# A second sequence's down projection as seven block products on one Trainium2 core, with their operand sums made in the stage before it

## The chip, the core and the metric

The program runs on one core of a Trainium2 chip. The core has five instruction queues that run side by side: TensorE (matrix products, called PE in the profile, with its weight loads as PEld), VectorE (DVE), ScalarE (ACT), GpSimd (POOL) and SyncE (SP), which here issues every transfer between the chip's memory and the on-chip buffers. The metric is the time of one execution on the device in microseconds (us), lower is better.

## The reference

One transformer-like layer is applied to two sequences, a sample of 512 tokens and a prompt of 1024 tokens, with the same weights (width 1024, feed-forward width 2816 = 22 x 128):

```python
def trunk(x, c, ...):
    ...
        mod = (c_act @ w_mod[l] + b_mod[l])[:, None, :]
        ...
        z = h @ w_in[l]
        ...
        mix = jnp.concatenate([rmsnorm(attn, g_attn_out[l]), rmsnorm(lru, g_lru_out[l])], axis=-1)
        x = x + gt1 * (mix @ w_out[l])
        h = rmsnorm(x, g_norm2[l]) * (1.0 + sc2) + sh2
        gu = h @ w_ffn_in[l]
        g_, u_ = jnp.split(gu, 2, axis=-1)
        x = x + gt2 * ((jax.nn.silu(g_) * u_) @ w_ffn_out[l])
    return rmsnorm(x, g_final)
```

The part that changes is the prompt's down projection `(silu(g) * u) @ w_ffn_out`, of size 1024 x 2816 x 1024, and what stands ahead of `mix @ w_out`.

## The kernel before

**Layout.** Activations stand transposed, features on the 128 partitions, tokens along the free side in chunks of 512: the sample is one chunk, the prompt two (0 and 1). A tile is 128x512. Every float32 matrix is split into a high and a low part of a rounded type (`whi`/`wlo` of a weight, `hh`/`hl`, `ach`/`acl`, `mxh`/`mxl` of activations), and one product of tiles is three matmuls (`mm3`): high by high, high by low, low by high. Making a high part is one copy on ScalarE (now and then on VectorE), a low part one subtraction on VectorE.

**Order.** Nothing is scheduled by the compiler. `Plan` (from line 90) keeps an estimated clock for each engine; `weave` (line 400) runs a main generator of matmuls and, at each of its yields, first emits drains that are due (`side.fast`), then the weight loader's steps (`pump`, line 338), then steps of background generators (`side.gens`) whose inputs the plan says are ready. `finish` (line 391) emits all that is left of a background generator before the main program goes on. What comes out is a fixed order on each engine, and each engine works through its own queue in order. `estimate` (line 99) gives the plan's costs: a float32 matmul of 512 columns counts 4 x 512 / 2400 = 0.853 us.

**Stages of the second half.** The sample's gate and up stage and the first half of its down projection (`ffn_out_half`) run while the prompt's recurrent unit (`lru`) and attention are worked off beside them. `s_lru` and `s_att` (lines 1524 and 1525) are two chains that end with `mix_lru` and `mix_att` of both prompt chunks: the squares of the four tiles are summed, `rstd` adds them over the partitions with two matmuls by `ones_h` (tiles `ssh`, `ssl`), then comes a root on ScalarE, four reciprocals on VectorE (`bc`), a scaling of each tile and its split into `mxh`, `mxl`. `side.finish(s_lru, s_att)` stands ahead of `out_main(1, 0, ...)`, the output projection of the prompt's chunk 0.

Then follow the output projections of chunks 0 and 1 (8 units of 24 matmuls each), the other half of the sample's down projection, and the prompt's gate and up stage `ffn_in_seven` (line 1239). It already multiplies by Strassen's scheme in Winograd's form: for each of 22 feature tiles j seven products of 12 matmuls make the gate and up tiles of both chunks; VectorE adds the products from PSUM, and the result tiles are stored to memory (`ac<-v`, `ac<-u`), 44 in all. Its seven right-hand operand sets (`ops`, 56 tiles) stay in a heap of 72 tiles (`N_HEAP`).

The prompt's down projection `ffn_out` (line 1371) then runs once for each chunk: 22 steps j, each with one weight tile pair (128x1024) and one activation tile, which `act_reader` loads and splits three steps ahead; 8 output tiles sit in 8 PSUM banks. `down` adds each output tile to the residual, squares it, and `final` (line 1421) normalises and stores. For chunk 1 the squares of the eight tiles are not summed on VectorE but given to TensorE as eight float32 matmuls by `ones_d`.

## Time and profile before

| what | us |
|---|---|
| median of 3 runs | 1638.21 (1635.48 to 1639.18) |
| the profiled execution, its own time | 1637.11 |
| its span, from the first instruction to the last | 1635.3 |
| TensorE busy | 1581.5 (97%) |
| VectorE busy | 1148.4 (70%) |
| ScalarE busy | 793.4 (49%) |
| prompt's gate and up stage (953.42 to 1373.48) | 420.06 |
| prompt's down projection (1373.48 to 1613.74) | 240.26 |

A matmul is listed with its latency (about 0.39 us), while the next one starts much earlier, so TensorE's busy time says that it had work, and the starts in the timeline say how fast it went. In tables by windows a number in parentheses is a count of instructions, PEclk is the granted TensorE clock as a share of full speed (0.50 is the lower level, 1.2 GHz of 2.4), and DMA is the mean busy share of the 16 DMA engines.

### The profile page before, as it was taken

The page shows a single profiled execution, that of the slowest core. Times are in us where ns is not written, and L with a number is a line of the kernel's source. Part 1 is how long each engine was busy: PE and PEld are TensorE (multiplying, and loading weights), DVE is VectorE, ACT ScalarE, POOL GpSimd, SP SyncE. Part 2 cuts the span into 40 slices and gives each one's busy share as a digit, 9 for nine tenths or more (in the row PEclk, how much of TensorE's full clock was granted, in tenths as well). Part 3 has the DMA queues.
Part 4 walks back from the last instruction along what each step waited for, and adds up shares of the span by engine and source line. Part 5 has one row for each costly group of instructions (what it writes and reads, how often), then busy time and mean ns, then how long its engine had stood idle before and what let it go on. Part 6 is the DMA issues. An engine that isn't in the chain of part 4 may idle for free.

```text
span 1635.3 us, 19943 instructions
## 1 busy us (share of the span) xinstructions
PE 1581.5 (97%) x7120; PEld 1273.0 (78%) x7120; DVE 1148.4 (70%) x1846; ACT 793.4 (49%) x1257; POOL 98.6 (6%) x148
## 2 busy tenths in 40 slices
PE   7999999999999999999699999999999999999996
PEld 1777888678678888888588888888888888888884
DVE  5787777637779897988857997666666666337334
ACT  3556786425985858665435643223222223334321
POOL 0000221000021120212000000000000000000000
PEclk9999999999999999999899999999999999999998
DMA  9674224475533333344365433222222226454541
GB/s 336 226 255 145 97 91 135 166 253 180 168 114 112 123 116 104 127 150 127 114 230 190 133 127 112 78 77 85 90 88 86 78 78 210 134 184 156 185 148 52
DMA packets 104787, 231.36 MB, mean 141 GB/s; under 512 B 10992, under 2 KB 17904, under 8 KB 104688
## 3 DMA queue, kind: packets, MB, share of 16 engines
q1 hardware_dynamic: 104688, 230.09, 42.6%
q8 instruction: 56, 0.92, 0.2%
q14 instruction: 43, 0.35, 0.1%
HBM read 189.16 MB, written 40.89 MB: 141 GB/s over the span
## 4 chain that ended last, share of the span: by engine, by line
PE 82%; ACT 7%; DVE 6%; DMA 2%; issue 2%; SPq 0%; DVEq 0%; ACTq 0%
PE pm L61 54%; PE ps L61 28%; ACT ga L61 2%; ACT gi L61 1%; ACT gs L61 1%; DMA mst<-w_mod 1%; DVE lh L61 1%; DVE bc L61 1%; DVE hl L61 1%; DVE x L61 1%; DVE wlo L61 0%; ACT L61 0%; SPq L61 0%; DVE ao L61 0%; DMA qf<-zq 0%
## 5 line engine op out<-in xcount | busy, mean ns | idle before, releaser
L61 PE MATMUL pm<-hh,whi 128*128 128x512 f32 x688 | 275.8, 401 | 0.2 <-DVE hh L61 0.2
L61 PE MATMUL pm<-hh,wlo 128*128 128x512 f32 x688 | 270.5, 393 | 2.1 <-DVE wlo L61 2.1
L61 PE MATMUL pm<-hl,whi 128*128 128x512 f32 x688 | 270.6, 393 | 0.5 <-DVE hl L61 0.5
L61 ACT ACTIVATE whi<-wst 128x1024 fp32r<-128x1024 f32 x134 | 141.2, 1056 | 210.7 <-PE pm L61 105.8
L61 DVE TENSOR_TENSOR wlo<-wst,whi 128x1024 fp32r<-128x1024 f32 x162 | 198.4, 1226 | 54.6 <-ACT whi L61 52.7
L61 PEld LDWEIGHTS pm<-hh,whi 128*128 128x128 f32 x688 | 130.6, 190 | 30.9 <-issue 4.4
L61 PEld LDWEIGHTS pm<-hh,wlo 128*128 128x128 f32 x688 | 130.3, 189 | 30.7 <-DVE wlo L61 2.5
L61 PEld LDWEIGHTS pm<-hl,whi 128*128 128x128 f32 x688 | 130.4, 190 | 25.9 <-DVE hl L61 1.1
L61 PE MATMUL pm<-ach,whi 128*128 128x512 f32 x352 | 138.3, 393 | 1.4 <-DVE sg L61 1.4
L61 PE MATMUL pm<-ach,wlo 128*128 128x512 f32 x352 | 137.1, 390 | 0.0
L61 PE MATMUL pm<-acl,whi 128*128 128x512 f32 x352 | 137.1, 390 | 0.0
L61 DVE TENSOR_TENSOR acl<-ac,ach 128x512 fp32r<-128x512 f32 x88 | 60.8, 696 | 81.9 <-ACT ach L61 80.8
L61 POOL TENSOR_SCALAR sx<-sx,es 128x384 f32<-128x384 f32 (+1 forms) x96 | 74.6, 794 | 255.5 <-DVE es L61 161.3
L61 ACT ACTIVATE ach<-ac 128x512 fp32r<-128x512 f32 x84 | 52.2, 628 | 64.4 <-DMA ac<-ac 62.8
L61 PEld LDWEIGHTS pm<-ach,whi 128*128 128x128 f32 x352 | 66.1, 188 | 15.2 <-DVE sg L61 1.8
L61 PEld LDWEIGHTS pm<-ach,wlo 128*128 128x128 f32 x352 | 66.1, 188 | 14.0
L61 PEld LDWEIGHTS pm<-acl,whi 128*128 128x128 f32 x352 | 66.1, 188 | 13.3 <-issue 0.2
L61 PE MATMUL pm<-mxh,whi 128*128 128x512 f32 x192 | 76.2, 397 | 0.0
L61 PE MATMUL pm<-mxl,whi 128*128 128x512 f32 x192 | 75.3, 392 | 0.0
L61 PE MATMUL pm<-mxh,wlo 128*128 128x512 f32 x192 | 75.3, 392 | 0.0
L61 DVE SCALAR_TENSOR_TENSOR x<-pm,modT,x 128x512 f32<-128x512 f32 x40 | 29.6, 745 | 56.8 <-PE pm L61 56.7
L61 PE MATMUL ps<-acl,whi 128*128 128x512 f32 x176 | 68.5, 389 | 0.0
(252 smaller groups left out, 3416.4 us busy)
## 6 DMA issues: line engine op xcount, KB each, us to landing
wst<-w_f SPq DMA_DIRECT2D x154, 512.0 KB, 3.7
mst<-w_mod SPq DMA_DIRECT2D x96, 256.0 KB, 5.4
ac<-ac SPq DMA_DIRECT2D x88, 256.0 KB, 4.1
wst<-w_in SPq DMA_DIRECT2D x28, 512.0 KB, 4.5
wst<-w_out SPq DMA_DIRECT2D x24, 512.0 KB, 3.7
x<-x_p SPq DMA_DIRECT2D x32, 256.0 KB, 5.5
xm<-x SPq DMA_DIRECT2D x24, 256.0 KB, 2.0
x<-xm SPq DMA_DIRECT2D x24, 256.0 KB, 6.0
```

Source lines behind the costliest of these rows:

```text
L61: r = fn(*args, **kw)
```

## The change

- **Down projection.** `ffn_out` is gone. `ffn_out_seven` computes both chunks at once by seven products: the 22 feature tiles are cut into two halves of 11, the 1024 outputs into two halves of 4 tiles. A product is 11 steps of 4 output tiles of 3 matmuls, 132 matmuls, into 4 PSUM banks (`pm` and `ps` in turn). After each product its four sums go to the residual tiles by VectorE (`p1` to `p7`).
- **Left sums.** `left_sums` is a background generator of the gate and up stage: for each of 11 pairs of weight tiles it loads four 128x512 blocks (`wd`), makes four sums on VectorE and stores them to memory (`s1`, `s2`, `d3`, `d4`), from where the last four products fetch them.
- **Right sums.** The gate and up stage goes through j in the order 0, 11, 1, 12, ... and after each pair `lean` makes four differences on VectorE (`t1` to `t4`); all seven right-hand sets go to memory, 77 tiles. `act_reader` reads them back four steps ahead.
- **Norms.** `s_lru` and `s_att` end with chunk 0's norm. Chunk 1's (`s_mix`) is made beside chunk 0's output projection, and finished ahead of chunk 1's.
- **End.** In the last product each output tile's squares are kept apart only for the last four tiles; the others are summed into one.
- **Plan.** A float32 matmul with 32 output rows (`mst,caw`, the modulation's product in strips) counts 0.15 us instead of 0.853.

The diff, cut to its core:

```diff
             four = op == "matmul" and kw["rhs"].dtype == F32
-            cost = max(4 * n, 515) / 2400 if four else max(n, 256 if op == "transpose" else 128) / 2400 + 0.0133 * (op == "matmul")
+            strip = four and outs[0].shape[0] == 32
+            cost = 0.15 if strip else max(4 * n, 515) / 2400 if four else max(n, 256 if op == "transpose" else 128) / 2400 + 0.0133 * (op == "matmul")
...
+            b[j // half, c] = d[v]
+            if j // half or c == 0:
+                yield d[v],
+                self.sp.dma_start(out=right[("11", "21")[j // half] if c == 0 else "22"][j % half], in_=d[v])
+            if key == (j % half + half, 1):
+                soon(lean(j % half, b[0, 0], b[0, 1], b[1, 0], b[1, 1]))
+
+        def lean(j, b11, b12, b21, b22):
+
+            yield b11, b12, b21, b22
+            t = {}
+            for n, x, y in (("t3", b22, b12), ("t1", b12, b11), ("t2", b22, "t1"), ("t4", b21, "t2")):
+                t[n] = self.T(n)
+                self.dve.tensor_tensor(out=t[n], in0=x, in1=t.get(y, y) if isinstance(y, str) else y, op=ALU.subtract)
+                yield t[n],
+                self.sp.dma_start(out=right[n][j], in_=t[n])
...
+        for j in (j for i in range(half) for j in (i, i + half)):
...
+    def left_sums(self, left):
+
+        def one(j):
+            a = []
+            for o in (0, NFF // 2):
+                for h in range(2):
+                    t = self.T("wd")
+                    self.sp.dma_start(out=t, in_=self.a["w_f2"][j + o, :, h * CH:(h + 1) * CH])
+                    a.append(t)
+            a11, a21, a12, a22 = a
...
+            yield a21, a22, a11
+            s3 = self.T("wd")
+            tt(out=s3, in0=a11, in1=a21, op=ALU.subtract)
+            yield s3,
+            store("d3", s3)
...
-    def ffn_out(self, seq, R, W, get, late, end, ahead, done):
+    def ffn_out_seven(self, seq, Rs, W, right, get, made, done):
...
+        def p7(m, ps, free):
+            yield lambda: at[m] == 6, ps
+            self.dve.tensor_tensor(out=u[m], in0=u[m], in1=ps, op=ALU.add)
+            free()
+            yield u[m],
+            onto(0, m + half, u[m])
+            yield from square(0, m + half)
+            left[0] -= 1
+            onto(1, m + half, u[m])
...
+        order = (("11", p1), ("21", p2), ("t4", p4), ("t2", p6), ("t3", p7), ("t1", p5), ("22", p3))
+        for p, (key, after) in enumerate(order):
...
+            cut = n - 3 if last else n - 1
+            if p == 2:
+                self.side.finish(made)
+            for j in range(cut):
+                take(j)
+                if p == 0 and j >= 2 and j - 2 < KT:
+                    for c in range(2):
+                        x[c][j - 2] = self.T("x")
+                        self.sp.dma_start(out=x[c][j - 2], in_=Rs[c]["dram"][j - 2])
+                for m in range(half):
+                    share(j, m)
...
-        s_lru = side.add(chain(self.lru(1, 2, zP, Lp, SQp), *(self.mix_lru(c, Lp, SQp, mixP[c]) for c in range(2))))
-        s_att = side.add(chain(self.attention(1, 2, zP, AOp), *(self.mix_att(c, AOp, mixP[c]) for c in range(2))))
+        s_lru = side.add(chain(self.lru(1, 2, zP, Lp, SQp), self.mix_lru(0, Lp, SQp, mixP[0])))
+        s_att = side.add(chain(self.attention(1, 2, zP, AOp), self.mix_att(0, AOp, mixP[0])))
...
         side.finish(s_lru, s_att)
+        s_mix = side.add(chain(self.mix_lru(1, Lp, SQp, mixP[1]), self.mix_att(1, AOp, mixP[1])))
         side.weave(out_main(1, 0, mixP[0], RP[0]))
+        side.finish(s_mix)
...
+        s_left.append(side.add(self.left_sums(left)))
+        side.weave(self.ffn_in_seven(W, ops, right, lambda: reads.append(self.act_reader(right["11"], 4))))
         ops.clear()
-        for c in range(2):
-            side.weave(self.ffn_out(1, RP[c], W, reads.pop(0), 2 * c, c == 1, read(1) if c == 0 else lambda: None, done_p(c)))
+        side.weave(self.ffn_out_seven(1, RP, W, right, reads.pop(), s_left[0], done_p))
```

How the orders move, at three places. First TensorE at the start of the prompt's output projection, before (`ach,whi` is the end of the sample's down projection, `ones_h` the sum of squares of a norm, `mxh,whi` the output projection):

```order
L61 MATMUL pm_6838<-ach_7574,whi_7339 128x512
L61 MATMUL pm_6838<-acl_7589,whi_7339 128x512
L61 MATMUL pm_6838<-ach_7574,wlo_7379 128x512
L61 MATMUL ps_7683<-ssh_7679,ones_h_91 128x512 [waits PE_49,Activation_49]
L61 MATMUL ps_7683<-ssl_7681,ones_h_91 128x512 [waits DVE_49]
L61 MATMUL pm_7726<-mxh_7652,whi_7425 128x512
L61 MATMUL pm_7726<-mxl_7660,whi_7425 128x512
```

The same place in the changed kernel:

```order
L61 MATMUL pm_6924<-ach_7607,whi_7418 128x512
L61 MATMUL pm_6924<-acl_7609,whi_7418 128x512
L61 MATMUL pm_6924<-ach_7607,wlo_7426 128x512
L61 MATMUL pm_7706<-mxh_7647,whi_7480 128x512 [waits DVE_49,Activation_49]
L61 MATMUL pm_7706<-mxl_7649,whi_7480 128x512
L61 MATMUL pm_7706<-mxh_7647,wlo_7495 128x512
L61 MATMUL pm_7706<-mxh_7651,whi_7480 128x512 [waits Activation_49]
L61 MATMUL pm_7706<-mxl_7660,whi_7480 128x512 [waits DVE_49]
```

The sum of squares of chunk 1's attention no longer stands ahead of the output projection; it comes 146 rows later, and the projection's first matmuls now wait for chunk 0's own split tiles.

Second VectorE in the middle of one feature tile of the prompt's gate and up stage, before (`u`, `v`, `w`, `p1` are sums of products, `slo`, `dlo`, `glo` low parts of weights, `wdif`, `wsum` weight sums):

```order
L61 TENSOR_TENSOR p1_9875<-p1_9875,ps_9903 128x512 [waits PE_49]
L61 TENSOR_TENSOR slo_9934<-wsum_9885,shi_9926 128x1024 [waits Activation_49]
L61 TENSOR_TENSOR w_9943<-u_9894,ps_9918 128x512 [waits DMAHW7_49,PE_49]
L61 TENSOR_TENSOR u_9894<-v_9910,ps_9918 128x512 [waits DVE_49]
L61 TENSOR_TENSOR wdif_9947<-wst_9821,wst_9835 128x512
```

The same place in the changed kernel, in the first part of that stage, with what now stands ahead of it:

```order
L61 TENSOR_TENSOR t2_9778<-u_9601,t1_9767 128x512 [waits DMAHW1_49,DVE_49]
L61 TENSOR_TENSOR t4_9788<-v_9628,t2_9778 128x512 [waits DMAHW3_49,DVE_49]
L61 TENSOR_TENSOR v_9791<-u_9769,ps_9757 128x512 [waits DMAHW4_49,PE_49]
L61 TENSOR_TENSOR wd_9793<-wd_9728,wd_9730 128x512 [waits DMAHW6_49,DMAHW5_49]
L61 TENSOR_TENSOR wd_9730<-wd_9730,wd_9734 128x512 [waits DMAHW0_49,DVE_49]
L61 TENSOR_TENSOR wd_9728<-wd_9730,wd_9728 128x512 [waits DVE_49]
L61 TENSOR_TENSOR p1_9745<-p1_9745,ps_9780 128x512 [waits PE_49]
L61 TENSOR_TENSOR wd_9732<-wd_9732,wd_9728 128x512 [waits DMAHW7_49,DVE_49]
L61 TENSOR_TENSOR slo_9823<-wsum_9747,shi_9813 128x1024 [waits Activation_49]
L61 TENSOR_TENSOR w_9841<-u_9769,pm_9805 128x512 [waits DMAHW2_49,PE_49]
```

Left sums and right differences stand between the sums of the products, and some of them wait for loads; here a feature tile is 17 instructions of VectorE's queue before and 25 now; the left sums are all made in the first nine of the 22 feature tiles, and after that a tile is 17 and 21 instructions in turn.

Third ScalarE at the end of the sample's norms, ahead of its output projection, before (`mrow` is the copy of a modulation row that TensorE waits for, `mxh` a high part for the output projection):

```order
L61 ACTIVATE mxh_2879<-lh_2376 128x512 [waits DMAHW6_49,DVE_49]
L61 ACTIVATE mrow_2887<-ps_2850 128x512 [waits DMAHW6_49,PE_49]
L61 ACTIVATE zo_2896<-pm_2817 128x512 [waits PE_49,Activation_49]
L61 ACTIVATE whi_2899<-wst_2218 128x1024
L61 ACTIVATE mxh_2901<-lh_2718 128x512 [waits DVE_49]
L61 ACT_TABLE_LOAD
L61 ACTIVATE bc_2903<-ps_2884,eps_93 128x512 [waits PE_49]
L61 ACTIVATE mxh_2963<-ao_1734 128x512 [waits DMAHW0_49,DVE_49]
```

The same place in the changed kernel:

```order
L61 ACTIVATE mxh_3022<-lh_2520 128x512 [waits DVE_49,Activation_49]
L61 ACTIVATE mxh_3032<-lh_2821 128x512 [waits DMAHW5_49,DVE_49]
L61 ACT_TABLE_LOAD [waits PE_49]
L61 ACTIVATE bc_3062<-ps_3049,eps_194 128x512 [waits Activation_49]
L61 ACT_TABLE_LOAD
L61 ACTIVATE zo_3082<-pm_2973 128x512
L61 ACTIVATE zo_3085<-pm_3040 128x512 [waits DMAHW7_49,PE_49]
L61 ACTIVATE mxh_3092<-ao_1852 128x512 [waits DVE_49,Activation_49]
```

The modulation's copy has moved ahead of the four `mxh<-lh`, and the attention's root and its table load now follow all four of them; on TensorE 18 matmuls stand between this norm's two matmuls by `ones_h` and the first matmul of the output projection, where before there were 48.

## Rows read from the trace of the kernel before

**Rows 1.** The page: span, TensorE's busy time, chain that ended last by engine.

```profile
span 1635.3 us, 19943 instructions
PE 1581.5 (97%) x7120; PEld 1273.0 (78%) x7120; DVE 1148.4 (70%) x1846; ACT 793.4 (49%) x1257; POOL 98.6 (6%) x148
PE 82%; ACT 7%; DVE 6%; DMA 2%; issue 2%; SPq 0%; DVEq 0%; ACTq 0%
```

**Rows 2.** Windows: length, busy PE, PEld, DVE, ACT, POOL; PEclk, DMA share, GB/s.

```profile
953.42:1373.48 420.06, 420.06 (x1850) 347.33 (x1851) 290.35 (x392) 127.35 (x165) 2.75 (x2) 1.00 0.29 94
1373.48:1613.74 240.26, 240.26 (x1059) 198.62 (x1058) 101.82 (x118) 78.49 (x99) 3.43 (x2) 1.00 0.47 153
900.00:940.00 40.00, 40.00 (x178) 33.14 (x177) 39.76 (x58) 26.90 (x42) 0.00 (x0) 1.00 0.40 130
```

**Rows 3.** TensorE's timeline at the end: start, length, instruction, count.

```profile
1613.52 0.39 PE L61 MATMUL ps<-ach,wlo 128*128 128x512 f32 x1
1613.74 7.03 PE L61 MATMUL ps<-sqt,ones_d 128*128 128x512 f32 x16
```

**Rows 4.** ScalarE's timeline at the end: the last tile's square.

```profile
1614.73 0.63 ACT L61 ACTIVATE sqt<-x 128x512 f32<-128x512 f32 x1 [2.03 <-DVE x L61]
```

**Rows 5.** TensorE's timeline at the prompt's output projection; in brackets the idle time before.

```profile
789.62 0.39 PE L61 MATMUL pm<-ach,wlo 128*128 128x512 f32 x1
802.36 0.79 PE L61 MATMUL ps<-ssh,ones_h 128*128 128x512 f32 x1 [12.35 <-ACT ssh L61]
803.68 0.63 PE L61 MATMUL pm<-mxh,whi 128*128 128x512 f32 x1
806.93 0.39 PE L61 MATMUL pm<-mxh,wlo 128*128 128x512 f32 x1
```

**Rows 6.** Windows of 5 us in that gap.

```profile
795.00:800.00 5.00, 0.00 (x0) 0.00 (x0) 4.30 (x8) 4.27 (x8) 0.00 (x0) 0.50 0.01 3
```

**Rows 7.** VectorE's timeline of chunk 0's attention norm.

```profile
780.06 0.69 DVE L61 TENSOR_TENSOR ssl<-sqt,ssh 128x512 fp32r<-128x512 f32 x1 [1.32 <-ACT ssh L61]
783.92 3.39 DVE L61 RECIPROCAL bc<-bc 128x128 f32<-128x128 f32 x4 [1.43 <-ACT bc L61]
789.09 2.73 DVE L61 SCALAR_TENSOR_TENSOR ao<-ao,vec,bc 128x512 f32<-128x512 f32 x4
796.96 2.49 DVE L61 TENSOR_TENSOR mxl<-ao,mxh 128x512 fp32r<-128x512 f32 x4
```

**Rows 8.** ScalarE's timeline of the same norm: table load and root.

```profile
781.90 1.28 ACT L61 ACT_TABLE_LOAD   x1 [1.35 <-PE ps L61]
783.19 0.69 ACT L61 ACTIVATE bc<-ps,eps 128x512 f32<-128x512 f32 x1
```

**Rows 9.** Who TensorE waited for, whole span: us in total, times, longest.

```profile
PE ps L61 <- ACT ssh L61: 12.4, 1, 12.4
PE ps L61 <- ACT mrow L61: 7.9, 4, 3.4
```

**Rows 10.** Windows of 6 us after two of the waits for `mrow`.

```profile
302.00:308.00 6.00, 6.00 (x18) 5.03 (x19) 5.04 (x9) 3.40 (x4) 0.00 (x0) 0.50 0.56 184
448.00:454.00 6.00, 6.00 (x25) 4.65 (x24) 5.96 (x14) 1.75 (x3) 2.79 (x4) 0.72 0.00 0
```

**Rows 11.** TensorE's timeline: one modulation product in strips, 8 matmuls as 16.

```profile
440.06 1.92 PE L61 MATMUL ps<-mst,caw 128*32 128x512 f32 x16
```

**Rows 12.** Groups by form, VectorE in the gate and up stage: busy, mean ns, idle.

```profile
L61 DVE TENSOR_TENSOR wsum<-wst 128x512 f32<-128x512 f32 x21 | 14.4, 684 | 0.0
L61 DVE TENSOR_TENSOR slo<-wsum,shi 128x1024 fp32r<-128x1024 f32 x21 | 25.6, 1220 | 0.5 <-ACT shi L61 0.5
```

**Rows 13.** DMA issues of the page: count, KB each, us to landing.

```profile
wst<-w_f SPq DMA_DIRECT2D x154, 512.0 KB, 3.7
ac<-ac SPq DMA_DIRECT2D x88, 256.0 KB, 4.1
```

**Rows 14.** A window at the start in which TensorE waited for loads.

```profile
20.00:40.00 20.00, 17.25 (x51) 4.71 (x49) 18.30 (x31) 3.06 (x5) 0.00 (x0) 0.97 0.98 365
```

More of the change, by code (lines that the diff above doesn't have):

```diff
@@ L1237, in ffn_in, with ffn_in_seven @@
                 W.free(*w)
-    def ffn_in_seven(self, W, ops, acts, ahead):
+    def ffn_in_seven(self, W, ops, right, ahead):
         def product(w, o, key):
@@ L1259, in add @@
         def add(d, ps, to, of):
-            d.setdefault(to, self.T(to) if to != of else d[of])
+            if to not in d:
+                d[to] = self.T(to)
             self.dve.tensor_tensor(out=d[to], in0=d[of], in1=ps, op=ALU.add)
@@ L1301, in ffn_in_seven @@
             W.free(*S)
[L1302 removed]
+            soon(gated(d, 6, *(yield from product((U, None), 0, "t4")), [("v", "v")], "p", "v", (j, 0)))
             W.free(U)
[L1304 removed]
+            soon(gated(d, 7, *(yield from product(D, 1, "22")), [("w", "w")], "w", "u", (j, 1)))
             W.free(*D)
@@ new lines, in left_sums @@
+    def left_sums(self, left):
[7 more added lines that the diff above has]
+            a11, a21, a12, a22 = a
+            tt = self.dve.tensor_tensor
+            sl = slice(j % 2 * CH, (j % 2 + 1) * CH)
+            store = lambda n, t: self.sp.dma_start(out=left[n][j // 2][:, sl], in_=t)
+            yield a21, a22, a11
[3 more added lines that the diff above has]
+            store("d3", s3)
+            tt(out=a21, in0=a21, in1=a22, op=ALU.add)
+            yield a21,
+            store("s1", a21)
+            tt(out=a11, in0=a21, in1=a11, op=ALU.subtract)
+            yield a11, a12
+            store("s2", a11)
+            tt(out=a12, in0=a12, in1=a11, op=ALU.subtract)
+            yield a12,
+            store("d4", a12)
+        for j in range(NFF // 2):
+            yield from one(j)
@@ L1455, in half_order, with down_order @@
             return [(("f2", p, i), two[i, :, :, p * CH:(p + 1) * CH]) for i in range(NFF // 2)]
-        f2 = [(("f2", j), a["w_f2"][j]) for j in range(NFF)]
+        n = NFF // 2
+        left = {k: [self.dram.tile([P, min(2, n - 2 * i) * CH], F32, name=f"{k}_{i}", tag=f"{k}_{i}") for i in range((n + 1) // 2)]
+                for k in ("s1", "s2", "d3", "d4")}
+        right = {k: [self.dram.tile([P, CH], F32, name=f"r{k}_{j}", tag=f"r{k}_{j}") for j in range(n)]
+                 for k in ("11", "21", "22", "t1", "t2", "t3", "t4")}
+        s_left = []
+        def down_order():
+            for p, (o, h) in enumerate(((0, 0), (n, 0), (n, 1))):
+                for i in range(0, n, 2):
+                    js = slice(o + i, o + min(i + 2, n))
+                    ap = a["w_f2"][js, :, h * CH:(h + 1) * CH].rearrange("j p m -> p j m")
+                    yield ("d", p, i // 2), W.plain(ap)
+            for p, k in enumerate(("s2", "d3", "s1", "d4")):
+                for i, t in enumerate(left[k]):
+                    yield ("d", 3 + p, i), W.plain(t, lambda: s_left and s_left[0] not in self.side.gens)
         W.order = [(key, W.plain(ap)) for key, ap in (
             wi + wi[:CUT] + wo + wi[CUT:] + f1_order + half_order(0) + wo + wo + half_order(1))]
-        W.order += [(("g", j), W.group(a["w_f1"][j], a["w_f1"][NFF + j])) for j in range(NFF)]
-        W.order += [(key, W.plain(ap)) for key, ap in f2 + f2]
+        W.order += [(("g", j), W.group(a["w_f1"][j], a["w_f1"][NFF + j])) for i in range(n) for j in (i, i + n)]
+        W.order += down_order()
         def chain(*gens):
@@ L1523, in program, with done_p, gen @@
         s_mod3 = side.add(mods(10, 11))
-        s_lru = side.add(chain(self.lru(1, 2, zP, Lp, SQp), *(self.mix_lru(c, Lp, SQp, mixP[c]) for c in range(2))))
-        s_att = side.add(chain(self.attention(1, 2, zP, AOp), *(self.mix_att(c, AOp, mixP[c]) for c in range(2))))
-        def done_p(c):
-            def done(tok, acc):
-                side.add(self.final(c, tok, RP[c], acc, a["y"][1]))
-                side.pace = side.most = 1
-                side.backlog = c == 0
-            return done
-        actS, actP = self.act_alloc(0, 1), self.act_alloc(1, 2)
+        s_lru = side.add(chain(self.lru(1, 2, zP, Lp, SQp), self.mix_lru(0, Lp, SQp, mixP[0])))
+        s_att = side.add(chain(self.attention(1, 2, zP, AOp), self.mix_att(0, AOp, mixP[0])))
+        def done_p(c, acc, when):
+            def gen():
+                yield when,
+                yield from self.final(c, slice(0, CH), RP[c], acc, a["y"][1])
+            side.add(gen())
+            side.pace = side.most = 1
+            side.backlog = c == 0
+        actS = self.act_alloc(0, 1)
         reads = []
-        read = lambda c: lambda: reads.append(self.act_reader(actP[c], 3))
         side.weave(self.ffn_in([RS], W, False, actS, lambda: reads.append(self.act_reader(actS[0], 4))))
```

165 lines of the change are left out of this document (107 added, 58 removed).

## The prediction

> **What bounds the kernel now.** I read the page first: TensorE is busy 97% of the span and holds 82% of the chain that ended last [rows 1]. Busy is not pace, so the next view is the windows of the two stages that the change touches. The prompt's down projection lasts 240.26 us [rows 2]. It is 2 x 22 x 8 x 3 = 1056 matmuls and one float32 matmul of `final`; the float32 ones take 7.03 / 8 = 0.88 us [rows 3], so the others go at (240.26 - 0.88) / 1056 = 0.2267 us. The gate and up stage, 22 x 7 x 12 = 1848 matmuls and one float32, comes to (420.06 - 0.88) / 1848 = 0.2268. Both run at the same pace at a granted clock of 1.00: TensorE never waits in either, and there only the number of matmuls counts. VectorE has room: 290 of 420 us and 102 of 240 [rows 2]. Third, the list of waits: one of 12.4 us for `ssh`, four for `mrow` that add up to 7.9 [rows 9]. Fourth, the timeline around them [rows 5 to 8, 10].
>
> **The sum is made against the profiled execution's own 1637.1 us;** the median of the three runs is 1638.2, 1.1 above it.
>
> **Term 1, fewer matmuls: -29.9 us.** Seven products of 132 are 924 matmuls instead of 1056. 132 x 0.2267 = 29.9. All of them lie on TensorE's path.
>
> Next to it stands a figure of the Trainium skill. The trace's spacing is 0.2267 us in both stages. The page "TensorE: Matmul & The Clock Gate", section "Back-to-back issue gap", gives 131 ns as the sustained spacing of 512-column matmuls in a stream with weight loads; by it this term would be 17.3 us and the time 1606. No stretch of this trace shows that spacing, so the measured 0.2267 stands.
>
> **Term 2, the end: -2.6 us.** After the last product TensorE adds 5 tiles of squares instead of 8 [rows 3]: 3 x 0.88. The last tile's square ends at 1615.36 [rows 4], 1.6 us after the sums begin, and the four others take 3.5, so the fifth doesn't wait. What follows is the same as before.
>
> **Term 3, the output projection: -12.3 us.** TensorE issues the last matmul of the sample's projection at 789.62, so it could go on at 789.85, and goes on at 802.36: 12.5 us. Then ten matmuls take 4.57 us until 806.93 instead of 2.27 [rows 5], since in the gap the granted clock fell to its lower level, 0.50 [rows 6]: 2.3 more, 14.8 in all. What is late is the norm of chunk 1's attention. Without it chunk 0's norm is the next to be late. I walk through it from the end of its `ssl`, 780.75. The reciprocals end 6.6 us after that [rows 7, 8]. In the new order VectorE then has a low part of an activation, one of a weight, four scalings (2.73), another weight's low part, and then the `mxl`; at 0.60 us for one 128x512 difference among several (2.49 for four) and 1.14 for a weight's, the four `mxl` end at 12.8, 14.1, 14.7 and 16.6. TensorE has 54 matmuls to do meanwhile and reaches the first tile at 13.2, the fourth tile's low part at 15.5: it waits 1.1 us. For chunk 1's own norm, made beside chunk 0's projection, the same walk with 48 matmuls between gives about 1.3 us at the start of chunk 1's. That is 2.5 of the 14.8 given back, too short to cost clock. Bounds: nothing given back (-14.8), or all of it, if chunk 0's norm takes as long as chunk 1's did (0). I take the walk.
>
> **Term 4, the plan's price of a strip: -2 us.** A modulation product in strips takes 1.92 us [rows 11], the plan booked 8 x 0.853 = 6.8. So the plan believed TensorE 5 us further on than it was and put `mrow` consumers too early; 7.9 us of waits, and 3.0 and 1.7 us of lost clock after two of them [rows 9, 10], 12.6 in all. With 0.15 most of it should go. But everything ahead of 790 us changes its order. The one place where I see a new wait is the sample's output projection: ScalarE now has four high parts, a table load and the root in a row, so I put the root 5.4 us after the norm's matmuls begin, the reciprocals at 8.8 and the first low part at 12.1, while TensorE, with 18 matmuls between, is there at 4.5. That is some 7.4 us of waits and 2.3 of clock, against the 6.4 that the `mrow` wait costs there now: +3.3. The other `mrow` waits cost 6.2 now. I take -2 and, for what an unread change of order may do, -9 to +7.
>
> **Term 5, VectorE in the gate and up stage: +2 us.** Added are 44 left sums and 44 right differences of 0.684 us [rows 12], 60 us to 290 in 420: on average there is room. But the left sums all fall in the first nine feature tiles. There VectorE has 9 x 13.3 for the tiles, 44 x 0.684 = 30.1, 16 differences 10.9, and `final` of the sample 8.1: 169 us in 9 x 84 x 0.2267 = 171. Two things make it lighter: in a row the instructions follow each other at 0.60 us rather than 0.69 [rows 7], about 18 us over 223 instructions; and between 900 and 940 us VectorE is busy for 39.76 of 40 us while TensorE keeps its pace [rows 2]. A drain has 7 products, 19 us, until its PSUM bank is wanted again. Bounds: 0, and the rival below. SyncE's queue gets 121 more issues in the stage, of which each store waits for its sum and holds the next load back; the weights are fetched about a tile (19 us) ahead and land in 3.7 us [rows 13], which covers that, and without the cover TensorE would pay each delay in full.
>
> **Term 6, transfers and drains in the down projection: +1.5 us.** In the first product SyncE issues 16 residual loads in 8 steps besides 8 activation and 4 weight tiles: 8.4 MB in 21.8 us, 385 GB/s, while the fullest window shows 365 with TensorE waiting [rows 14]. At 365 this takes 23.0 us, 1.2 late; four steps of prefetch (10.9 us) against 4.1 us of landing [rows 13] and two splits hide some of it. Each later product ends in a burst on VectorE, up to 16 instructions, some 12 us, with the next product's fifth split behind it; TensorE wants it 12.9 us after the burst begins. In the last product the tenth load stands behind a store of chunk 0's output and is due with about 1 us to spare. Bounds 0 and 7.
>
> The page "DMA: Bandwidth & Descriptors", section "Specifications", puts a core's limit to memory at about 358 GB/s, which would make the first product 1.6 us late instead of 1.2; the window of 365 GB/s lies above it.
>
> **Sum:** -29.9 - 2.6 - 12.3 - 2 + 2 + 1.5 = -43.3, so 1637.1 - 43.3 = **1593.8, say 1594 us**. With the bounds of terms 3 to 6 mixed, this case's own range is 1584 to 1603.
>
> **The rivals.**
>
> *VectorE falls behind in the first nine tiles.* Its sums wait in order for loads that SyncE issues late. If each of the 11 sets of left sums holds the queue for 3 us, 33 us go into some 19 of room; TensorE then pays 14 and 2 to 4 of lower clock: 1594 - 2 + 17 = 1609. For it: rows of `wd` wait for loads issued right behind a store. Against: the plan lets six us pass between load and sum. Chance 0.12.
>
> *Terms 3 and 4 bring nothing.* Chunk 0's norm and the changed order take the place of the waits removed: 1594 + 14.3 = 1608. For it: VectorE is nearly full in that stretch, and the sample's projection gets such a wait. Chance 0.11.
>
> *Slower than before, by SyncE's queue in the gate and up stage.* Weight loads stand behind stores that wait for VectorE. If each of the 22 tiles gets its weights late, TensorE loses that much 22 times and, by the gap at 790 us, more on the lower clock; from 43.3 / 22 = 2.0 us per tile the whole gain is gone, and at 3 us it ends at 1594 + 66 = 1660. Against it: the tile's lead of 19 us. Chance 0.04.
>
> **How the numbers follow.** The forecast has 0.72, the rivals 0.27, and 0.01 is left for others. A measurement of this kernel can tell about 0.2%, 3 us, from no change. The forecast and the rivals but one are faster: 0.94; within 0.2% 0.02; slower 0.04. A range of 1584 to 1610 holds nearly all of the forecast and most of the rivals that end at 1608 and 1609.
>
> **What would show it.** The changed profile should show the seven products in about 210 to 212 us at a clock of 1.00, the gate and up stage in 420 to 423 with VectorE busy for about 350 us, most densely in its first 170; no wait of over 3 us for `ssh` at the prompt's output projection; five `sqt` sums at the end in 4.4 us; `mrow` waits below 4 us in all, and a wait of 5 us or more for `mxh` or `mxl` at the sample's. I would be wrong by term 5 if the gate and up stage is over 430 us, by term 6 if the products take over 218, by terms 3 and 4 if the prompt's gate and up stage doesn't begin some 14 us earlier than before.

## The result, and the profile after

The changed kernel takes 1591.87 us (median of 4 runs, 1589.49 to 1592.35) against 1636.85 (4 runs, 1634.47 to 1639.18): a ratio of 0.9722, 95% interval 0.9703 to 0.9741, or 45 us. The forecast was 1594, the range 1584 to 1610. The profiled execution of the changed kernel is the fastest of its four, 1589.49 us with a span of 1587.7, so the traces differ by 47.6 us where the medians differ by 45.0.

The page (answers to [rows 1]): span, busy time, and the chain that ended last by engine.

```profile
span 1587.7 us, 20208 instructions
PE 1545.2 (97%) x6982; PEld 1242.2 (78%) x6982; DVE 1224.4 (77%) x1989; ACT 810.5 (51%) x1299; POOL 90.9 (6%) x148
PE 85%; DVE 6%; ACT 5%; issue 2%; DMA 2%; SPq 0%; POOL 0%; DVEq 0%; ACTq 0%; POOLq 0%
```

TensorE has as large a share of the span as before. VectorE's has gone from 70 to 77%, with 76 us more work in a shorter program. The windows (columns as in [rows 2]): the gate and up stage, its first 170 us, the seven products, and the first of them.

```profile
936.48:1357.01 420.53, 420.27 (x1851) 347.37 (x1851) 339.68 (x477) 127.21 (x166) 2.84 (x2) 1.00 0.50 166
936.48:1106.48 170.00, 169.74 (x745) 139.88 (x746) 157.34 (x228) 52.19 (x69) 2.84 (x2) 1.00 0.72 244
1357.01:1568.67 211.66, 210.90 (x927) 173.74 (x926) 134.96 (x182) 92.19 (x134) 2.76 (x2) 1.00 0.59 206
1357.01:1387.10 30.09, 30.08 (x133) 24.59 (x131) 15.80 (x21) 11.35 (x17) 0.00 (x0) 1.00 0.99 362
```

The gate and up stage has 49 us more VectorE work and hardly grows; the products run at the old pace.

TensorE's timeline at three places: the start of the prompt's output projection (answers to [rows 5]), the step from the first product to the second, and the end (answers to [rows 3]).

```profile
780.43 0.39 PE L61 MATMUL pm<-ach,wlo 128*128 128x512 f32 x1
781.02 0.47 PE L61 MATMUL pm<-mxh,whi 128*128 128x512 f32 x1 [0.21 <-DVE x L61]
...
784.05 0.50 PE L61 MATMUL pm<-mxl,whi 128*128 128x512 f32 x1 [0.52 <-DVE mxl L61]
...
830.88 0.50 PE L61 MATMUL pm<-mxl,whi 128*128 128x512 f32 x1 [1.87 <-DVE mxl L61]
...
1386.70 0.39 PE L61 MATMUL pm<-ach,wlo 128*128 128x512 f32 x1
1387.62 0.49 PE L61 MATMUL ps<-ach,whi 128*128 128x512 f32 x1 [0.53 <-ACT ach L61]
1388.34 0.50 PE L61 MATMUL ps<-acl,whi 128*128 128x512 f32 x1 [0.23 <-DVE acl L61]
...
1568.67 4.45 PE L61 MATMUL ps<-sqt,ones_d 128*128 128x512 f32 x10
```

The gap of 12.35 us is gone. Small waits for `mxl` have come, at chunk 0's start (784) and at chunk 1's (831). From 1386.70 to 1388.68 three matmuls take 1.98 us instead of 0.68, 1.3 us too long; it is the one delay inside the products.

TensorE's waits over the whole span (answers to [rows 9]; `ssh` is no longer among them):

```profile
PE pm L61 <- DVE mxl L61: 4.2, 4, 1.9
PE pm L61 <- ACT mxh L61: 2.9, 1, 2.9
...
PE ps L61 <- ACT mrow L61: 2.1, 2, 1.4
```

The 47.6 us by stage, each boundary a start in the timeline (the last matmul ahead of the output projection, the first one behind it, and so on):

| stretch | before | after | difference |
|---|---|---|---|
| start to the prompt's output projection | 789.62 | 780.43 | -9.19 |
| output projection of both chunks | 103.06 | 95.31 | -7.75 |
| other half of the sample's down projection | 60.74 | 60.74 | 0 |
| gate and up stage | 420.06 | 420.53 | +0.47 |
| down projection | 240.26 | 211.66 | -28.60 |
| after it | 21.56 | 19.03 | -2.53 |

Read like this, the plan's price of a strip seems to have brought 9 us ahead of the output projection, and the divided norms 8 us in it. The runs below show that this reading is wrong.

### The profile page after: what moved, and what is told of

Read it like the earlier page. It is cut to its first block, busy times and chain, and to the rows that moved or that the text cites. A ratio compares the mean times of both kernels' runs of the same rounds, so it can differ in the third digit from the quotient of the medians.

```text
span 1587.7 us, 20208 instructions
## 1 busy us (share of the span) xinstructions
PE 1545.2 (97%) x6982; PEld 1242.2 (78%) x6982; DVE 1224.4 (77%) x1989; ACT 810.5 (51%) x1299; POOL 90.9 (6%) x148
## 4 chain that ended last, share of the span: by engine, by line
PE 85%; DVE 6%; ACT 5%; issue 2%; DMA 2%; SPq 0%; POOL 0%; DVEq 0%; ACTq 0%; POOLq 0%
PE pm L61 57%; PE ps L61 27%; ACT ga L61 2%; ACT gi L61 1%; DMA mst<-w_mod 1%; DVE bc L61 1%; ACT gs L61 1%; DVE x L61 0%; DVE wlo L61 0%; DVE sqt L61 0%; DVE yo L61 0%; ACT whi L61 0%; DVE mxl L61 0%; SPq L61 0%; DMA kf<-zk 0%
## 5 line engine op out<-in xcount | busy, mean ns | idle before, releaser
L61 DVE TENSOR_TENSOR wlo<-wst,whi 128x1024 fp32r<-128x1024 f32 (+1 forms) x160 | 191.9, 1201 | 30.3 <-ACT whi L61 28.8
L61 DVE TENSOR_TENSOR acl<-ac,ach 128x512 fp32r<-128x512 f32 x121 | 80.9, 690 | 39.9 <-ACT ach L61 39.6
L61 ACT ACTIVATE ach<-ac 128x512 fp32r<-128x512 f32 x118 | 72.1, 626 | 71.9 <-DMA ac<-rt 28.2
L61 POOL TENSOR_SCALAR sx<-sx,es 128x384 f32<-128x384 f32 (+1 forms) x96 | 68.2, 728 | 234.4 <-DVE es L61 131.8
L61 DVE RECIPROCAL bc<-bc 128x128 f32<-128x128 f32 (+1 forms) x57 | 51.1, 953 | 22.7 <-ACT bc L61 22.7
L61 ACT ACTIVATE dhi<-wdif 128x1024 fp32r<-128x1024 f32 x22 | 23.4, 1063 | 86.9 <-DVE wdif L61 38.0
```

The lines of the kernel that those rows point to most:

```text
L61: r = fn(*args, **kw)
```

## Experiments

"Undone" is the changed kernel without one part, "alone" the kernel before with only that part. Ratios are to the kernel before in the same session, with 95% intervals.

| run | median us | ratio |
|---|---|---|
| the change | 1591.87 | 0.9722 (0.9703 to 0.9741) |
| price_alone | 1636.50 | 0.9999 (0.9987 to 1.0011) |
| norms_alone | 1621.64 | 0.9903 (0.9885 to 0.9921) |
| seven_alone | 1606.46 | 0.9811 (0.9793 to 0.9829) |
| price_undone | 1589.67 | 0.9709 (0.9692 to 0.9727) |
| norms_undone | 1605.32 | 0.9806 (0.9785 to 0.9828) |
| lru_early | 1599.54 | 0.9769 (0.9753 to 0.9785) |
| left_double | 1612.49 | 0.9847 (0.9832 to 0.9861) |
| left_triple | 1646.64 | 1.0058 (1.0043 to 1.0073) |
| best | 1587.79 | 0.9698 (0.9683 to 0.9712) |
| price_lead2 | 1586.96 | 0.9691 (0.9676 to 0.9706) |
| true_lead5 | 1594.28 | 0.9730 (0.9716 to 0.9745) |
| all_mends | 1583.60 | 0.9673 (0.9660 to 0.9686) |

### The three parts, each by itself

**price_alone**: the kernel before with

```diff
-            cost = max(4 * n, 515) / 2400 if four else ...
+            strip = four and outs[0].shape[0] == 32
+            cost = 0.15 if strip else max(4 * n, 515) / 2400 if four else ...
```

> The kernel before with one line of the change: the plan books a strip matmul at 0.15 us instead of 0.853. Theory after the result: the stretch ahead of the prompt's output projection is 9.2 us shorter in the changed kernel's trace, and all of that comes from the price, so this kernel ends 9 us below the kernel before (about 1628 against 1637). The prediction's term 4 put it at -2 (1635). Rival: the norm split and the price act together, since both move the same VectorE work, and the price alone brings nothing or less than 3 us because the 12.4 us wait for chunk 1's norm takes up what is won ahead of it. The trace is to show mrow waits of about 2 us instead of 7.9 in every case.

Measured: no change, within 2 us. The rival holds. TensorE's timeline ahead of the output projection:

```profile
785.84 0.39 PE L61 MATMUL pm<-ach,wlo 128*128 128x512 f32 x1
801.05 0.79 PE L61 MATMUL ps<-ssh,ones_h 128*128 128x512 f32 x1 [14.83 <-ACT ssh L61]
```

TensorE arrives 3.8 us earlier than before [rows 5] and then waits 2.5 us longer; the output projection behind it ends 0.6 us earlier than before, and nothing of it is left in the medians. The `mrow` waits are gone (2.1 us are left), but what they cost was not on the way to the end: the norm behind them is ready only 1.3 us earlier (801.05 instead of 802.36), so TensorE mostly waits longer there.

**norms_alone**: the kernel before with

```diff
-        s_lru = side.add(chain(self.lru(1, 2, ...), *(self.mix_lru(c, ...) for c in range(2))))
-        s_att = side.add(chain(self.attention(1, 2, ...), *(self.mix_att(c, ...) for c in range(2))))
+        s_lru = side.add(chain(self.lru(1, 2, ...), self.mix_lru(0, ...)))
+        s_att = side.add(chain(self.attention(1, 2, ...), self.mix_att(0, ...)))
...
+        s_mix = side.add(chain(self.mix_lru(1, ...), self.mix_att(1, ...)))
         side.weave(out_main(1, 0, mixP[0], RP[0]))
+        side.finish(s_mix)
```

> The kernel before with only the norms divided: chunk 1's two norms are made beside chunk 0's output projection. Theory after the result: the output projection gets 7.7 us shorter, 4 of the 14.8 being given back at chunk 1's start, so about 1629 against 1637. The prediction's term 3 put it at -12.3 (1624.5). Rival: the order ahead of it decides, and with the old price chunk 0's own norm is late as well: less than 4 us gained, above 1633.

Measured: -0.97%, some 16 us (the interval reaches from 13 to 19), more than any of the three said. **price_undone** is the changed kernel with the first diff taken back:

> The changed kernel with the old price of a strip, 0.853 us. Theory: the 9.2 us ahead of the output projection are lost again: about 1601 against the changed kernel's 1592, mrow waits back at about 8 us. The prediction's term 4 gives 1594. Rival: with the norms divided the wait that the price saves is hidden, and nothing changes (1592).

Measured: 1589.67. Its interval overlaps with the change's, so whether the new price costs some 2 us or nothing stays open; a gain of 9 us, as the theory has it, is excluded. The output projection of both chunks in one window each (length, busy PE, PEld, DVE, ACT, POOL, PEclk, DMA, GB/s), first the changed kernel:

```profile
780.43:875.74 95.31, 92.06 (x392) 74.14 (x391) 79.46 (x108) 49.76 (x74) 0.00 (x0) 0.98 0.57 191
```

and with the old price:

```profile
786.50:875.25 88.75, 88.75 (x393) 73.39 (x391) 76.70 (x104) 48.57 (x72) 0.00 (x0) 1.00 0.58 200
```

With the old price TensorE comes to the output projection 6.1 us later and goes through it without one wait, in 88.75 us (norms_alone also: 786.88 to 875.63). With the new one it comes earlier and loses 6.56 us in it, and both leave at about the same time, 875.25 and 875.74. But 1.7 of the 6.1 us were there long before, where TensorE has issued the same first 300 matmuls in both; first the changed kernel's timeline, then the one with the old price:

```profile
92.00 0.39 PE L61 MATMUL pm<-hh,wlo 128*128 128x512 f32 x1
...
93.72 0.39 PE L61 MATMUL pm<-hh,wlo 128*128 128x512 f32 x1
```

So the price brings TensorE some 4 us earlier to a place where 6.56 are lost. That is a cost of some 2 us, as the medians have it, but two executions of one order can differ by nearly as much (best, below, has price_undone's order up to there and comes at 788.02).

The divided norms are worth 103.06 - 88.75 = 14.3 us there, all of the gap and its low clock: two matmuls of chunk 1's norms, 0.45 us, stand in this stretch besides, which makes the prediction's 14.8.

**seven_alone**: the changed kernel with both small parts undone.

> The changed kernel with the price and the norm split both undone: the seven products alone. Theory: the gate and up stage, the down projection and the end give -30.6 as in the changed kernel's trace, so about 1606 against 1637, with the gate and up stage at 420.5 us, the products at 211.7 and the wait for the reload of 1.2 us at the start of the second product. The prediction's terms 1, 2, 5 and 6 give -29.0 (1608). Rival: the stage after depends on where the order ahead leaves VectorE, and the gate and up stage stalls: above 1612.

Measured: 1606.46, as the theory said (1606): gate and up stage 420.50 us, products 211.63, the rest 19.06. The down projection's part doesn't depend on the order ahead of it.

**norms_undone**: the changed kernel with the second diff taken back.

> The changed kernel with the norm split undone: both chunks' norms are finished ahead of chunk 0's output projection again, with the new price of a strip. Theory: the wait for ssh is back with 12 to 15 us and its lower clock, and the time is the one of the seven products alone, 1606. Rival: the new order ahead makes that norm early enough, and less than 8 us are lost (below 1600).

Measured: 1605.32, the time of the seven products alone. TensorE's timeline:

```profile
784.71 0.39 PE L61 MATMUL pm<-ach,wlo 128*128 128x512 f32 x1
799.92 0.80 PE L61 MATMUL ps<-ssh,ones_h 128*128 128x512 f32 x1 [14.82 <-ACT ssh L61]
```

The gain of the change is that of two parts that add up: 0.9811 x 0.9903 = 0.9716, and 0.9709 was measured for both without the price.

### Why the price brings nothing

With the new price the plan's clock of TensorE is less far ahead, and it issues the background work later among the matmuls: between the squares' sum of chunk 0's attention and the output projection stand 54 matmuls in the changed kernel and 102 in price_undone, and for chunk 1 48 and 66 (counted in the traces). Either that order is the cause, or VectorE and ScalarE do that stretch's work no earlier whatever the order.

**lru_early**: one of chunk 1's two norms is made ahead again.

```diff
-        s_lru = side.add(chain(self.lru(1, 2, ...), self.mix_lru(0, ...)))
+        s_lru = side.add(chain(self.lru(1, 2, ...), *(self.mix_lru(c, ...) for c in range(2))))
...
-        s_mix = side.add(chain(self.mix_lru(1, ...), self.mix_att(1, ...)))
+        s_mix = side.add(self.mix_att(1, ...))
```

> The changed kernel, but only the attention's norm of chunk 1 is made beside chunk 0's output projection; the recurrent unit's norm of chunk 1 stays where it was before the change, ahead of it. Theory A: the new price brings TensorE to the output projection 6 us earlier, and the time is lost again only because two norms of chunk 1 stand behind each other in 192 matmuls; with one of them made earlier the waits of 3.1 us and the 1.6 us of low clock around chunk 1's start go, and the time is about 1587. Rival B: VectorE and ScalarE are what sets the time up to there, and the norm put ahead makes chunk 0's own norm as much later: 1590 to 1594, with a wait of 4 us or more for mxh or mxl at chunk 0's start.

Measured: 1599.54, worse than either said; in kind it is the rival. Chunk 1's start loses its waits, and chunk 0's gets a longer one:

```profile
785.71 0.39 PE L61 MATMUL pm<-ach,wlo 128*128 128x512 f32 x1
794.27 0.80 PE L61 MATMUL pm<-mxh,whi 128*128 128x512 f32 x1 [8.18 <-ACT mxh L61]
796.20 0.79 PE L61 MATMUL pm<-mxl,whi 128*128 128x512 f32 x1 [1.13 <-DVE mxl L61]
```

So a norm that is put ahead of the output projection is paid there. This fits the rival, but the order changed as well (12 matmuls instead of 54 ahead of chunk 0's projection), so it doesn't decide. **price_lead2** changes the order alone: the changed kernel with

```diff
+        def lead():
+            self.plan.at["pe"] += 2.0
+            return
+            yield
+
-        s_mod3 = side.add(mods(10, 11))
+        s_mod3 = side.add(chain(mods(10, 11), lead()))
```

> The changed kernel with one addition in the plan: when the last strip products have been issued (mods 10 and 11, at about 440 us), the plan's clock of TensorE is set 2 us ahead once. Nothing else is edited; the order it gives has 90 matmuls between the squares' sum of chunk 0's attention and the output projection where the changed kernel has 54, and 90 between that of chunk 1 and its projection where it has 48; the start up to 440 us is the same. Theory A: the new price does take TensorE's waits away up to there, but it also lets the plan issue the background work later, so that both norms come late; with the order put back, what is won ahead stays: the output projection takes 88.5 to 89 us instead of 95.3 and the time is about 1586. Rival B: VectorE and ScalarE do that stretch's work no earlier whatever the order, so that the same waits appear somewhere between 440 us and the output projection: 1590 to 1593.

In its trace 90 matmuls stand ahead of chunk 0's projection, as expected, and 66 ahead of chunk 1's, not 90.

Measured: 1586.96, the output projection in one window:

```profile
784.68:873.43 88.75, 88.75 (x392) 73.40 (x391) 76.70 (x104) 48.46 (x72) 0.00 (x0) 1.00 0.58 200
```

Theory A holds for the output projection: with the order put back, the 6.56 us are not paid there although the price is the new one. Nor are they a chance of one execution: left_double and left_triple (below) have the changed kernel's order up to there, TensorE comes at 783.03 and 782.54, and the projection takes 95.27 us in both. The rival has a share: ahead of it stand new waits, the longest this one in TensorE's timeline,

```profile
566.01 0.66 PE L61 MATMUL ps<-ident,sx 128*128 128x128 f32 x4 [1.88 <-ACT gi L61]
```

and TensorE reaches the output projection 4.2 us later than in the changed kernel, 1.75 of which arise in the first 45 us, where both issue the same order (last section). So some 2.5 of the 6.56 us turn up elsewhere, and some 4 are won.

**true_lead5** books the strip at 0.24 us, its measured time, and uses a lead of 5:

```diff
-            cost = 0.15 if strip else ...
+            cost = 0.24 if strip else ...
...
+            self.plan.at["pe"] += 5.0
```

> The changed kernel with the strip booked at 0.24 us, which is what the trace shows for one (1.92 / 8), instead of 0.15, and the plan's clock of TensorE set 5 us ahead once after the last strips. In the order it gives there are 54 matmuls between the last norm's sum and the sample's output projection where the changed kernel has 18, and 102 ahead of chunk 0's projection. Theory A: the sample's projection loses its waits for mxh and mxl of 4.3 us and 1.7 us of low clock, the prompt's loses 6.6 us, and the time is about 1580. Rival B, that VectorE and ScalarE set the pace up to the output projection: 1588 to 1592.

Measured: 1594.28; theory A is wrong at the sample's output projection. TensorE's timeline there, and at a new place:

```profile
307.70 0.80 PE L61 MATMUL pm<-mxh,whi 128*128 128x512 f32 x1 [3.67 <-ACT mxh L61]
309.57 0.79 PE L61 MATMUL pm<-mxl,whi 128*128 128x512 f32 x1 [1.07 <-DVE mxl L61]
...
449.51 0.33 PE L61 MATMUL ps<-ident,sx 128*128 128x128 f32 x1 [3.97 <-POOL sx L61]
```

The sample's waits are as long as in the changed kernel (3.67 and 1.07 us, there 2.94 and 1.36), although 54 matmuls instead of 18 stand ahead of them. VectorE's timeline shows why: two norms stand in a row there, and VectorE works without a pause from 293.58 to 311.25. Below it the last line of the same work in the changed kernel:

```profile
293.58 4.19 DVE L61 RECIPROCAL bc<-bc 128x128 f32<-128x128 f32 x5
297.69 1.16 DVE L61 TENSOR_TENSOR wlo<-wst,whi 128x1024 fp32r<-128x1024 f32 x1
...
306.18 2.73 DVE L61 SCALAR_TENSOR_TENSOR ao<-ao,vec,bc 128x512 f32<-128x512 f32 x4
308.84 2.48 DVE L61 TENSOR_TENSOR mxl<-ao,mxh 128x512 fp32r<-128x512 f32 x4
```

```profile
308.29 2.49 DVE L61 TENSOR_TENSOR mxl<-ao,mxh 128x512 fp32r<-128x512 f32 x4
```

In both orders the last low parts are ready at about 311 us: at the sample's projection VectorE's work is the bound. At the prompt's the order is: here too that projection takes 88.75 us without a wait, but TensorE comes to it only at 790.08, behind new waits of which the 3.97 us above is the longest. A price closer to the truth did not give a better order here; the price and the lead were changed together, so which of them brings the new waits stays open.

### How near VectorE is to its limit in the gate and up stage

**left_double** and **left_triple** repeat the first left sum of each pair 4 and 8 times more:

```diff
             tt(out=s3, in0=a11, in1=a21, op=ALU.subtract)
+            for _ in range(4):
+                self.tc.nc.vector.tensor_tensor(out=s3, in0=a11, in1=a21, op=ALU.subtract)
```

> The changed kernel with each pair's first left sum made five times over (four more VectorE subtractions of 128x512 with the same result), unknown to the plan, so that VectorE's work for the left sums doubles: 44 x 0.60 = 26.5 us more in the stage's first nine feature tiles. Theory: VectorE is busy for 157 of the stage's first 170 us, so 12.7 us fit, the other 14 are carried along as lag, and a drain may lag 19 us before its PSUM bank is wanted: 0 to +3 us (1592 to 1595), the stage at 421 to 424 us. Rival, the prediction's first one: VectorE's lag reaches TensorE at once through the weight sums, and the stage grows by about 14 us and the lower clock: 1606 to 1610.

> As the kernel with the left sums doubled, with eight more subtractions for each pair instead of four: 88 x 0.60 = 53 us more. Theory: 40 us over the room, 19 of them carried as lag, so TensorE pays about 21 us and 2 to 4 us of lower clock: 1613 to 1618. Rival: without any carried lag it pays all 40 and more (1632 or above). If neither this nor the doubled kernel moves, VectorE's busy time is no measure of its room.

Measured: 1612.49 and 1646.64. My own theory of a lag that is carried along fell; the rival held in kind, and the loss is larger than it said. The windows of the dense stretch, first left_double:

```profile
939.04:1129.04 190.00, 177.42 (x745) 142.52 (x746) 181.49 (x263) 51.46 (x68) 2.83 (x2) 0.97 0.62 211
```

then left_triple:

```profile
938.55:1178.55 240.00, 201.65 (x810) 158.69 (x811) 226.82 (x329) 56.75 (x75) 2.82 (x2) 0.91 0.53 179
```

and left_double's extra subtractions in VectorE's timeline:

```profile
1052.25 2.87 DVE L1410 TENSOR_TENSOR wd<-wd 128x512 f32<-128x512 f32 x4
```

Eleven times 2.87 us are 31.6 us of added work, 63.1 in left_triple. TensorE idles 190 - 177.42 = 12.6 us and 240 - 201.65 = 38.4; so 19 us fit in the first case and 25 in the second. The stage grows by 20.3 (420.53 to 440.82) and 55.3 us. Of what goes beyond the idle time, 7.7 and 17, some 6 and 13 are matmuls that start more than 0.2267 us apart with no wait between them, at a lower granted clock (0.97 and 0.91 on average); the rest stands at the waits themselves. TensorE's waits, left_double:

```profile
PE pm L61 <- ACT dhi L61: 4.5, 2, 2.9
...
PE ps L61 <- ACT dhi L61: 3.3, 2, 2.5
PE ps L61 <- DVE dlo L61: 2.5, 2, 1.3
```

They are for the weight differences `dhi` and `dlo`, not for PSUM banks: the weight sums stand in VectorE's queue among the drains, and the next product wants them before the bank of a late drain is wanted.

### Two small mends, and all together

**best** is price_undone with two edits in the down projection:

```diff
-                if p == 0 and j >= 2 and j - 2 < KT:
-                    for c in range(2):
-                        x[c][j - 2] = self.T("x")
-                        self.sp.dma_start(out=x[c][j - 2], in_=Rs[c]["dram"][j - 2])
+                if p < 2 and j >= 2 and j - 2 < KT:
+                    x[p][j - 2] = self.T("x")
+                    self.sp.dma_start(out=x[p][j - 2], in_=Rs[p]["dram"][j - 2])
...
-            yield from square(1, m, True)
+            yield from square(1, m, m > 1)
```

> The changed kernel with the old price of a strip and two edits in the down projection. First, the residual of chunk 1 is loaded in the second product instead of the first: the start of the second product, which waits 1.2 us for its activations now, should lose that wait. Second, in the last product the squares of the first two tiles are summed on VectorE too, so that three float32 matmuls end the program instead of five: 2 x 0.88 = 1.8 us less. Theory: 1589.7 - 1.2 - 1.8 = 1586.7. Rivals: the late reload isn't caused by the residual loads, and the wait stays (1588); the summed squares arrive after TensorE and it waits for them (1587 to 1588).

Measured: 1587.79. The window of the products and TensorE's timeline at the end:

```profile
1358.00:1568.34 210.34, 210.34 (x927) 173.81 (x926) 136.73 (x184) 93.05 (x134) 2.77 (x2) 1.00 0.60 207
```

```profile
1568.34 2.85 PE L61 MATMUL ps<-sqt,ones_d 128*128 128x512 f32 x6
```

The products take 210.34 us instead of 211.66, and from the last of them to the end 17.5 instead of 19.0 (three float32 matmuls, listed as six, instead of five): -1.3 and -1.5, each at the place of its edit. The median is 1.1 above the 1586.7 expected, within the spread of the runs.

**all_mends** adds the same two edits to price_lead2.

> The kernel with TensorE's clock in the plan set 2 us ahead after the strips, with the two edits in the down projection added: the residual of chunk 1 is loaded in the second product, and three float32 matmuls end the program instead of five. Theory: the three edits act at different places and add up: 1587.0 - 1.3 - 1.6 = 1584 us, 3% below the kernel before; products 210.3 us, the tail 17.4 us. Rival: the later stages are led by VectorE's order and the gains of the end don't add up: 1586 or above.

Measured: 1583.60, ratio 0.9673 (0.9660 to 0.9686), the fastest kernel here; its products take 210.34 us and what follows 17.4, as expected. It differs from best in the new price with its lead alone, by 4.2 us; price_lead2 and price_undone differ by the same, by 2.7. The intervals of both pairs overlap, so a small gain of price and lead together is likely but not shown.

## Why the prediction was right, and where it wasn't

The sum was -43.3 and the medians say -45.0. Four terms held one by one; two, the norms and the price, were wrong in opposite directions, and that they cancel in the sum is luck.

- **Term 1 (-29.9)** held. Without any wait the products take 210.34 us, and 924 x 0.2267 + 0.88 is 210.35. The spacing that the Trainium skill gives ("TensorE: Matmul & The Clock Gate", section "Back-to-back issue gap", 131 ns) is not seen in this stream either.
- **Term 6 (+1.5)** held in place and cause: 211.66 - 210.34 = 1.3 us, at the start of the second product. That the residual loads cause it is shown by the kernel that spreads them and loses the delay. No later product is late. That the size comes so near is in part luck: the 365 GB/s of [rows 14] are the mean of 20 us and no limit, for shorter windows of the first product go above it, and the term's list of transfers leaves out four stores of the last right sums (`rt<-t`).

```profile
1367.00:1372.00 5.00, 5.00 (x24) 4.14 (x23) 1.92 (x2) 1.86 (x3) 0.00 (x0) 1.00 1.06 400
```

  The window of the whole first product shows 362 GB/s, just above the 358 of the Trainium skill's page "DMA: Bandwidth & Descriptors", section "Specifications".
- **Term 2 (-2.6)** held: 21.56 to 19.03 is -2.5, five sums in 4.45 us where eight took 7.03 [rows 3].
- **Term 5 (+2)** measured +0.5, VectorE busy for 340 us instead of about 350. But the cover named for it, 19 us until a bank is wanted, was the wrong one: the weight differences come due first. The rival's "some 19 of room" happened to be right (31.6 us added, 12.6 paid in idle time); for the 2 to 4 us that it put on the clock, left_double pays 7.7 beyond the idle time.
- **Term 3 (-12.3)** was too small for the edit and too large for the changed kernel. The edit alone gives the whole gap, -14.3 us in the trace, with nothing given back. In the changed kernel 6.56 us are given back, not 2.5. The walk to chunk 0's start was right: 1.1 us predicted, 1.2 measured. The step that failed is "the same walk ... gives about 1.3 us at the start of chunk 1's": of the 6.56 us, some 5 are lost around it, by waits and by the lower clock behind them. VectorE's timeline there:

```profile
827.53 0.75 DVE L61 SCALAR_TENSOR_TENSOR x<-pm,modT,x 128x512 f32<-128x512 f32 x1
829.53 0.69 DVE L61 TENSOR_TENSOR sqt<-sqt 128x512 f32<-128x512 f32 x1 [1.25 <-ACT sqt L61]
830.14 1.89 DVE L61 TENSOR_TENSOR mxl<-ao,mxh 128x512 fp32r<-128x512 f32 x3
```

  and ScalarE's:

```profile
826.88 1.06 ACT L61 ACTIVATE whi<-wst 128x1024 fp32r<-128x1024 f32 x1 [1.79 <-PE pm L61]
827.84 1.13 ACT L61 ACTIVATE mxh<-ao 128x512 fp32r<-128x512 f32 x2
828.88 0.61 ACT L61 ACTIVATE sqt<-x 128x512 f32<-128x512 f32 x1
```

  Chunk 0's output tiles are drained and squared here (`x`, `sqt`) while chunk 1's norm is made. ScalarE makes a weight's high part first, the square comes late, VectorE's sum waits 1.25 us for it, and three `mxl` stand behind that sum. The walk names no such drains. The waits are longer than the walk's 1.3 us and also cost clock: the window 830 to 835 shows a granted clock of 0.68, which is 5 x 0.32 = 1.6 us.
- **Term 4 (-2)** is 0 by itself, and in company 0 or a small loss. What it expected in the trace came: `mrow` waits of 2.1 us instead of 7.9 [rows 9], and waits at the sample's projection, 4.3 us where 7.4 were foreseen, none of them the 5 us or more named as a sign. The step that failed is to book the saved waits as time: what is won counts only if the work that TensorE meets next is earlier too. It came 3.8 us earlier in price_alone and some 4 in the changed kernel, and lost that again at the output projection, in the first by waiting 2.5 us longer for the same norm, in the second by the order that the new price gives.
- Together, terms 3 and 4 were -14.3 and the stretch up to the gate and up stage is 16.9 shorter, 2.3 of it from the start of the two profiled executions (last section). So the sum was right although neither term was: term 3 by itself is 2 us short, term 4 is 2 us over, and the loss at chunk 1's start was offset by the earlier arrival.

The rivals: VectorE doesn't fall behind in the nine tiles as the kernel stands, but 31.6 us more of work does it. Terms 3 and 4 together did not come to nothing; term 4 alone did. SyncE's queue made nothing late in the gate and up stage.

## What to carry to other kernels

A stretch that is shorter in the trace is not yet a gain: follow it to the next place where TensorE waits, and undo each part by itself before the time won at a place is credited to an edit. Where several engines are driven in an order fixed beforehand, look for what stands in the queue of the slower engine ahead of the wanted work (here a sum that waits for a square), and give that engine's own queue, not the buffers, as the measure of its room. When a stage is dense on a second engine, doubling its added work for one run shows the room in microseconds.

## What was not expected of the hardware

The granted clock at the start differs between executions of the same instructions. The changed kernel and price_lead2 issue the same order up to 440 us, and in both TensorE waits 2.1 us for a `wlo` at 37 us. From 35 to 45 us the window of the first shows

```profile
35.00:45.00 10.00, 7.92 (x34) 5.32 (x34) 8.18 (x14) 5.61 (x9) 0.00 (x0) 1.00 0.85 289
```

and the second

```profile
35.00:45.00 10.00, 7.93 (x28) 4.31 (x27) 6.62 (x12) 5.13 (x9) 0.00 (x0) 0.83 0.88 296
```

a clock of 1.00 in one and 0.83 in the other, which is 1.5 to 1.7 us. The kernel before also shows 0.83 there, and so do left_double and left_triple, which issue the changed kernel's order. What decides it no run shows. By 70 us, with TensorE's order still the same in both, the kernel before is 2.3 us behind the changed one (0.75 of it by its first waits for loads): so 2.3 of the 9.19 us that the two traces differ by ahead of the output projection belong to no edit. And four subtractions that write the same tile in a row take 0.72 us each (2.87 for four), where differences into different tiles took 0.60 [rows 7]. It is not only for the same result: right behind them stand two sums of which the second reads the tile that the first has written, and they too start 0.73 us apart (the second takes 0.69):

```profile
1055.15 1.42 DVE L61 TENSOR_TENSOR wd<-wd 128x512 f32<-128x512 f32 x2
```
